# A two-block transformer kernel: stepped norm and late low-rank finishing in block one, 96-row products in block two

## The chip, the cores and the metric

The kernel runs on one core of one Trainium2 chip. The metric is the device time of one execution in microseconds, lower is better. The engines: TensorE (PE, with its weight loads as PEld), VectorE (DVE), ScalarE (ACT), GpSimd (POOL) and SyncE (SP), which only issues DMAs here. ACT and POOL can issue DMAs too.

## The reference, cut to what matters

Two transformer blocks run one after the other on x of 1024 tokens by 1024 columns, in float32. What the change touches of block one:

```
h = rms_norm(x, norm_in)
proj = h @ w_in            # dq dk dv dgate cq ckv kr mgate g_diff g_mla
cq = rms_norm(cq, mla_q_norm)             # 384 columns
q = cq @ w_uq              # 4 heads: 128 plain, 64 rotated columns
ckv = rms_norm(ckv, mla_kv_norm)          # 256 columns
kv = ckv @ w_ukv           # 4 heads: 128 of k, 128 of v
k_rope = apply_rope(kr, cos, sin)         # 64 columns for all heads
```

Two causal attentions over q, k, v follow, gated with silu(dgate) and silu(mgate). What it touches of block two (a recurrence over tokens beside a dilated attention, then a feed-forward part):

```
logw = -softplus(-(w0 + tanh(xw) @ w_up)) - 0.5     # xw: 32 columns
a = sigmoid(a0 + xa @ a_up)                         # xa: 32 columns
g = sigmoid(xg) @ g_up                              # xg: 96 columns
```

## The kernel before, in words

Every large product is taken in three: a float32 operand is split into a rounded part (hi) and the rest (lo), and `mm3` (L196) adds hi x hi, hi x lo and lo x hi in one PSUM bank. `split` (L174) makes hi on ACT and lo on DVE; with a gain it multiplies by it on the way. Weights pass through a raw tile (`wr`, two buffers) that SP loads, and a split tile (`w`, four buffers).

`block_one` (L442) first norms x. In each of two halves of 512 tokens, four tiles of 128 tokens are loaded on SP, their sums of squares taken on ACT (`sumsq`, L435), the reciprocal root on DVE and POOL (`rstd`, L167), and the tiles scaled on DVE (L466). `to_T` (L257) then makes, for each of 8 blocks of 128 columns, four PE transposes into one PSUM bank, from which ACT writes hi (L269) and DVE writes lo (L270) of hT. The banks for transposes follow `tp_tags` (L446): one bank "tp" and, twice in three, one of the two banks "pj", which the products use too.

`attention_one` (L484) then makes, in this order: the rope tables (L310, DVE and ACT's sine); lambda (four small loads, DVE and ACT's exponential, L501 to L512); the split weights Wc of cq and Wk of ckv and kr; the products for cq (L568), eight token blocks of 128 tokens with 8 x 3 products each (`proj_tok_steps`, L212); those for ckv and kr (L577); the gate of the second attention (`gate_tok(1)`, L534); then q's rotated part (`qrope`, L595), q and k of four heads and v (L609 to L614), which `spill` (L601) copies from PSUM to a tile `ev` (two buffers, pool `evs`) and SP stores in DRAM. Each block of cq and ckv goes through `finish` (L556): copy from PSUM on DVE (L165), sum of squares, norm (L562). After every fourth block `finish` calls `to_T` for all four tiles at once, with the norm's gain taken in at L269 and L270. After that come the products for the first heads and the attention, in which two streams of instructions are woven so that PE has products of the one while the other waits.

In block two `project_two` projects into the recurrence's inputs. It makes T (L1000 to L1007), 128 partitions of 1024 tokens: rows 0 to 31 tanh(xw) rounded, 32 to 63 its rest, 64 to 95 and 96 to 127 the same of xa. `rwkv_tokens` (L1017), run for four groups of 128 channels, loads the `up` weights (L1027 to L1033), splits them, and `up` (L1044) multiplies 64 rows of T with the rounded weights (twice the same 32 rows) and 32 rows with the rest: two products of 64 and 32 partitions in one bank, for decay (rows from 0) and for a (rows from 64), for each half of the tokens.

The order of instructions on each engine is set when the kernel is built. In block one, the order of the program gives the priority, and an instruction comes in when what it needs is ready by a model of the times. In block two (`run`, L1911), a planner orders the whole block by a simulated timeline. `weave` (L115) takes turns between two streams by their stated costs.

Of the kernel before, what the change touches and what calls it, by code (L numbers as in the profile page):

```python
# [86 lines left out]
class Build:  # L87
# [288 lines left out]
    def q_stack(self, x, m):  # L376

        nc = self.nc
        qs = self.work.tile([128, 2, 2, 2, 64], F32R, name="qs")
# [5 lines left out]
        def rest():  # L385
# [5 lines left out]
            q = self.work.tile([128, 2, 2, 128], F32R, name="qT")  # L391
# [50 lines left out]
    def block_one(self):  # L442
        nc, A, tc = self.nc, self.A, self.tc
        with ExitStack() as st:
            self.psum = self.pool(st, "ps1", bufs=2, space=PSUM)
            self.tp_tags = ["tp", "pj", "pj"]  # L446
# [6 lines left out]
            with tc.tile_pool(name="xa", bufs=8, reuse_waits="tile") as xp:  # L453
                cm = xp.tile([128, 128], F32, name="cm", bufs=1)
# [29 lines left out]
    def attention_one(self, st, hT):  # L484
        nc, A, tc = self.nc, self.A, self.tc
        self.rope_tables(self.pool(st, "rope"))
# [12 lines left out]


        lam = self.consts.tile([128, 1], F32, name="lam")  # L501
        lq = self.work.tile([128, 4, 64], F32, name="rp1")
        for i, n in enumerate(("diff_lambda_q1", "diff_lambda_k1", "diff_lambda_q2", "diff_lambda_k2")):
            nc.sync.dma_start(lq[:, i], rows(A[n]))
# [1444 lines left out]
```

## Time and profile before

| | us |
|---|---|
| median of 3 runs | 2550.12 |
| lowest and highest | 2544.97, 2550.53 |
| the profiled execution's own time | 2538.74 |
| its span in the trace | 2536.5 |
| PE busy in the span | 2380.1 (94%) |
| DVE, ACT, POOL busy | 1495.4 (59%), 1018.2 (40%), 284.7 (11%) |
| mean granted TensorE clock | 0.976 |

The busy share is a mean over stages with different limits. A wait matters where it is PE's; idle time of the other engines costs nothing by itself. In the trace's names "pj<-w,hT_hi" is a product into a tile pj from tiles w and hT_hi, and L199 is the line that issues it.

### The profile page before, as it was taken

Reading aid. Unit: us, or ns where it says so; the run is one execution under the profiler, and the core shown is the slowest. Engines: PE = TensorE matmul, PEld = TensorE weight load, DVE = VectorE, ACT = ScalarE, POOL = GpSimd, SP = SyncE. Lnnn points to the kernel's source line nnn. Section 1 sums busy time; section 2 is a strip of 40 time slices with the busy share of each in tenths; the row PEclk is TensorE's granted clock in tenths of the full one; section 3 lists DMA queues with packets and bytes.
Section 4 is the critical chain, followed back from the end, with each engine's and each line's share of the span. In section 5 each row is a group of like instructions: output and inputs, shape, how many; then the busy total and the mean of one; then the engine's idle time right before and its main releaser. Section 6 shows DMA issues by size and latency. Waiting matters only on the chain.

```text
span 2536.5 us, 38731 instructions
## 1 busy us (share of the span) xinstructions
PE 2380.1 (94%) x14288; PEld 2087.0 (82%) x14288; DVE 1495.4 (59%) x3183; ACT 1018.2 (40%) x2210; POOL 284.7 (11%) x678
## 2 busy tenths in 40 slices
PE   7898999999999899899998798989999999989997
PEld 6887999898887689778797788988997877778776
DVE  5432457454445644466474265757667666688888
ACT  4312344344443225333342254445666444433333
POOL 1000000000001000101111554531100000000001
PEclk9999999999999999899999898999999999999999
DMA  3134222222213531335367676543556444443222
GB/s 112 52 110 138 81 61 80 64 76 76 73 63 125 179 138 53 76 75 165 96 185 206 173 165 173 157 119 96 178 160 183 144 138 133 170 133 109 74 76 107
DMA packets 371597, 302.47 MB, mean 119 GB/s; under 512 B 126161, under 2 KB 305233, under 8 KB 371409
## 3 DMA queue, kind: packets, MB, share of 16 engines
q1 hardware_dynamic: 345296, 271.69, 36.1%
q10 hardware_dynamic: 25472, 26.22, 3.6%
q8 instruction: 113, 1.85, 0.3%
q0 software_dynamic: 640, 2.10, 0.2%
q14 instruction: 76, 0.61, 0.1%
HBM read 208.69 MB, written 91.23 MB: 118 GB/s over the span
## 4 chain that ended last, share of the span: by engine, by line
PE 68%; DMA 11%; DVE 9%; ACT 4%; issue 3%; POOL 3%; SPq 2%; ACTq 0%; DVEq 0%; POOLq 0%
PE pj L199 34%; PE x L199 7%; PE z L199 5%; PE y L199 4%; PE pv L426 4%; DMA wr<-w_ffn_up 3%; PE tp L254 3%; DVE w L181 2%; ACT w L163 1%; PE sc L686 1%; POOL U L1262 1%; POOL Ut L1260 1%; DMA v<-bkv_t 1%; DMA Al<-at_d 1%; PE Z L1314 1%
## 5 line engine op out<-in xcount | busy, mean ns | idle before, releaser
L199 PE MATMUL pj<-w,hT_hi 128*128 128x256 f32 (+2 forms) x2560 | 539.8, 305 | 17.6 <-ACT w L177 7.4
L199 PEld LDWEIGHTS pj<-w,hT_hi 128*128 128x128 f32 x2560 | 420.6, 192 | 27.0 <-ACT w L177 7.7
L199 PE MATMUL pj<-hT_hi,w 128*128 128x512 f32 (+1 forms) x1216 | 395.4, 400 | 10.3 <-DVE tg L830 7.2
L199 PE MATMUL pj<-w,hT_lo 128*128 128x256 f32 (+2 forms) x1280 | 383.8, 301 | 0.0
L181 DVE TENSOR_TENSOR w<-wr,w 128x1024 fp32r<-128x1024 f32 (+4 forms) x349 | 279.2, 826 | 138.8 <-ACT w L163 136.6
L163 ACT ACTIVATE w<-wr 128x1024 fp32r<-128x1024 f32 (+4 forms) x345 | 241.5, 736 | 253.4 <-PE z L199 66.4
L199 PEld LDWEIGHTS pj<-hT_hi,w 128*128 128x128 f32 (+1 forms) x1216 | 228.1, 189 | 62.5 <-ACT w L163 6.6
L199 PEld LDWEIGHTS pj<-w,hT_lo 128*128 128x128 f32 x1280 | 245.9, 192 | 0.6 <-issue 0.5
L199 PE MATMUL pj<-hT_lo,w 128*128 128x512 f32 (+1 forms) x608 | 241.9, 398 | 0.0
L172 POOL TENSOR_TENSOR rstd<-rs_t,mhalf 128x1 f32<-128x1 f32 x88 | 59.3, 679 | 1511.9 <-DVE rs_t L171 1462.6
L199 PE MATMUL z<-w 128*128 128x512 f32 x720 | 166.9, 392 | 4.7 <-DVE c L1824 3.7
L199 PE MATMUL y<-w 128*128 128x512 f32 x624 | 150.5, 400 | 14.6 <-ACT w L163 9.4
L199 PEld LDWEIGHTS z<-w 128*128 128x128 f32 x720 | 135.7, 189 | 34.5 <-issue 4.1
L199 PEld LDWEIGHTS y<-w 128*128 128x128 f32 x624 | 119.9, 194 | 43.9 <-ACT w L163 10.7
L199 PE MATMUL ua<-T,w 128*128 128x512 f32 x576 | 139.5, 393 | 6.8 <-DVE o L1756 3.6
L199 PEld LDWEIGHTS ua<-T,w 128*128 128x128 f32 x576 | 107.3, 188 | 33.9 <-issue 8.0
L199 PEld LDWEIGHTS pj<-hT_lo,w 128*128 128x128 f32 (+1 forms) x608 | 115.4, 190 | 23.1 <-issue 0.8
L403 DVE TENSOR_REDUCE mx<-sc 128x1 f32<-128x128 f32 (+7 forms) x96 | 70.8, 754 | 101.6 <-PE sc L411 101.1
L254 PE MATMUL tp<-ident,p 128*128 128x128 f32 x576 | 98.5, 278 | 7.2 <-ACT pt L163 6.2
L199 PE MATMUL x<-w,mix_hi 128*128 128x256 f32 x512 | 92.3, 284 | 0.0
L199 PE MATMUL x<-B,w 128*128 128x512 f32 x384 | 88.3, 390 | 0.0
L407 ACT ACTIVATE p<-sc,mx 128x128 f32<-128x128 f32 (+7 forms) x96 | 70.7, 740 | 36.1 <-DVE mx L404 34.2
(440 smaller groups left out, 4391.2 us busy)
## 6 DMA issues: line engine op xcount, KB each, us to landing
wr<-w_ffn_up SPq DMA_DIRECT2D x48, 512.0 KB, 4.8
wr<-u_d SPq DMA_DIRECT2D x32, 512.0 KB, 5.2
wr<-w_ffn_down SPq DMA_DIRECT2D x32, 512.0 KB, 4.9
wr<-w_in SPq DMA_DIRECT2D x28, 512.0 KB, 4.1
wr<-w_in_first SPq DMA_DIRECT2D x192, 64.0 KB, 2.0
u_d<-o SPq DMA_DIRECT2D x48, 256.0 KB, 3.8
tg<-tg_d SPq DMA_DIRECT2D x32, 256.0 KB, 3.0
x_d<-x SPq DMA_DIRECT2D x16, 512.0 KB, 3.7
```

Source lines behind the costliest of these rows:

```text
L163: self.nc.scalar.activation(out, in_, AF.Copy)
L172: nc.gpsimd.tensor_tensor(out, t, self.mhalf[:, :ss.shape[-1]], op=OP.pow)
L181: self.nc.vector.tensor_sub(lo, x, hi.bitcast(F32))
L199: self.nc.tensor.matmul(ps, a, b, start=start, stop=stop, **({"skip_group_check": True} if onto else {}))
L254: self.nc.tensor.transpose(tp[:, j * 128:j * 128 + 128], s, ident)
L403: nc.vector.tensor_reduce(mx, sc[:, :n], axis=AX, op=OP.max)
L407: nc.scalar.activation(p[:, :n], sc[:, :n], AF.Exp, bias=mx, scale=scale, accum_out=s)
L426: self.nc.tensor.matmul(o[:, :w], pts[j], V[:, j], start=j == 0, stop=j == nb - 1)
L686: nc.tensor.matmul(o, qn, KN[:, c0:c0 + w], start=True, stop=False)
L1260: nc.gpsimd.tensor_mul(tmp[:, :ni, :w], U[:, :ni, s:s + 1].to_broadcast([128, ni, w]), Al[:, s:s + 1, s + 1:].to_broadcast([128, ni, w]))
L1262: nc.gpsimd.tensor_sub(U[:, :ni, s + 1:], U[:, :ni, s + 1:], tmp[:, :ni, :w])
L1314: mm(ps[:, j * 128:j * 128 + 128], lhs(c), rhs(c, j), start=True, stop=True)
```

## The change

In block one, all eight x tiles are asked for at the start, four on SP's queue and four on ACT's. Only half 0 is normed and transposed first. The rest of the norm is a generator, `second`, that is advanced once after each token block of cq: the norm of two tiles, that of the other two, the transposes of four column blocks, those of the other four, then the causal mask's load. The rope tables follow after block 4, lambda after ckv. Transposes now use the one bank "tp" and the one bank "pv" by turns. `finish` returns a generator: its first step is the norm's multiplication, its second the transposes of this one block (three for cq, two for ckv, in one bank, then hi on ACT and lo on DVE). `proj_tok_steps` keeps such generators in a list and advances each once after every later token block; the list is handed from cq to ckv and to the gate. The gains of both norms are taken into the weights' split. Spills and `qrope` use a pool `lev` with five buffers of `ev` in place of `evs`. The attention's tiles qs, qT, gt and mo move to a second pool, `work2`; rope's and mla's pools change sides.

In block two, T is made in a scratch tile and four DMAs copy it into two tiles of 96 partitions (hi, lo, hi again). The weights are loaded three times (32 rows each; two rounded, one turned into the rest), so that `up` is one product of 96 partitions. The split of these weights is one ACT and two DVE instructions instead of two and two.

```diff
@@ to_T
-        for d in range(nd):
+        for d in range(d0, d0 + nd):
             def then(i, n, ps, d=d):
-                hi = hT[0][:, d0 + d, half * 512:half * 512 + 512]
-                lo = hT[1][:, d0 + d, half * 512:half * 512 + 512]
+                hi = hT[0][:, d, half * 512:half * 512 + 512]
+                lo = hT[1][:, d, half * 512:half * 512 + 512]
...
@@ block_one
-            self.tp_tags = ["tp", "pj", "pj"]
+            self.tp_tags = ["tp", "pv"]
...
+            slow, sx = ExitStack(), ExitStack()
+            low = self.pool(slow, "low")
+            xp = self.pool(sx, "xa", bufs=8)
+            xs = [xp.tile([128, D], F32, name="x") for _ in range(NT)]
+            for t in range(NT):
+                (nc.sync if t < 4 else nc.scalar).dma_start(xs[t], A["x"][0, t * 128:t * 128 + 128, :])
+
+            def norm(ts):
+                for t in ts:
+                    ss = self.small.tile([128, 1], F32, name="ss")
+                    self.sumsq(t, ss, D)
+                    r = self.norm_rows(ss, D)
+                    nc.vector.tensor_scalar(t, t, r, None, op0=OP.mult)
+
+            def second():
+
+                norm(xs[4:6])
+                yield
+                norm(xs[6:8])
+                yield
+                for d in (0, 4):
+                    self.to_T(xs[4:8], hT, 1, 4, lambda d: gain[:, d:d + 1], d)
+                    yield
+                cm = self.work.tile([128, 128], F32, name="kx")
                 nc.sync.dma_start(cm, A["c_causal"])
                 nc.vector.tensor_copy(self.causal, cm)
-                for half in range(2):
-                    ts = []
-                    for j in range(4):
-                        t = xp.tile([128, D], F32, name="x")
-                        r0 = (half * 4 + j) * 128
-                        nc.sync.dma_start(t, A["x"][0, r0:r0 + 128, :])
-                        ss = self.small.tile([128, 1], F32, name="ss")
-                        self.sumsq(t, ss, D)
-                        r = self.norm_rows(ss, D)
-                        nc.vector.tensor_scalar(t, t, r, None, op0=OP.mult)
-                        ts.append(t)
-                    self.to_T(ts, hT, half, 8, lambda d: gain[:, d:d + 1])
-            if "hT" in self.dbg:
-                for i in range(2):
-                    nc.sync.dma_start(self.dbg["hT"][i], hT[i].bitcast(F32))
-                return
-            self.attention_one(st, hT)
+                sx.close()
...
+            norm(xs[0:4])
+            self.to_T(xs[0:4], hT, 0, 8, lambda d: gain[:, d:d + 1])
+            self.attention_one(st, hT, second(), slow, low)
...
@@ attention_one
-        self.rope_tables(self.pool(st, "rope"))
...
+        def minus_lambda():
+            lq = self.work.tile([128, 4, 64], F32, name="rp1")
...
-                self.split(t[:, 0], t[:, 1], raw)
+                self.split(t[:, 0], t[:, 1], raw, None if gain is None else gain[:, k:k + 1])
...
+        mla = self.pool(st, "mla", side="right")
+        self.rpool = self.pool(st, "rope", side="right")
...
+            def finish(width, dst, tb, ps):
+
+                t = low.tile([128, 384], F32, name="c", bufs=5)[:, :width]
+                self.evac(t, ps[:, :width], "v")
+                ss = self.small.tile([128, 1], F32, name="ss")
+                self.sumsq(t, ss, width)
+                r = self.norm_rows(ss, width)
+                n, sl = width // 128, slice(tb * 128, tb * 128 + 128)
+
+                def then(i, k, ps):
+                    ps = ps.rearrange("p (d t) -> p d t", d=n)
+                    nc.scalar.activation(dst[0][:, :, sl], ps, AF.Copy)
+                    nc.vector.tensor_sub(dst[1][:, :, sl], ps, dst[0][:, :, sl].bitcast(F32))
+
+                def rest():
+                    nc.vector.tensor_scalar(t, t, r, None, op0=OP.mult)
+                    yield
+                    self.transposes([t[:, d * 128:d * 128 + 128] for d in range(n)], then)
+                return rest()
+
+            late = []
+            for tb, _ in enumerate(self.proj_tok_steps(hT, Wc, 384, lambda tb, ps: finish(384, cqT, tb, ps), late=late)):
+                next(second, None)
+                if tb == 4:
+                    self.rope_tables(self.rpool)
             Wk = w_cols(320, 2432)
-            group = []
-
-            def finish(width, gain, dst, tb, ps):
-                t = low.tile([128, 384], F32, name="c", bufs=5)
-                self.evac(t[:, :width], ps[:, :width], "v")
-                ss = self.small.tile([128, 1], F32, name="ss")
-                self.sumsq(t[:, :width], ss, width)
-                r = self.norm_rows(ss, width)
-                nc.vector.tensor_scalar(t[:, :width], t[:, :width], r, None, op0=OP.mult)
-                group.append(t)
-                if len(group) == 4:
-                    self.to_T(list(group), dst, tb // 4, width // 128, lambda d: gain[:, d:d + 1])
-                    group.clear()
-
-            self.proj_tok(hT, Wc, 384, lambda tb, ps: finish(384, qn_gain, cqT, tb, ps))
+            low2 = self.pool(s2, "low2")
+            ckT = [low2.tile([128, 2, S], F32R, name=n) for n in ("ck_hi", "ck_lo")]
...
+                g = finish(256, ckT, tb, ps)
+
+                def rest():
+                    next(g)
+                    stack()
+                    yield
+                    next(g, None)
+                return rest()
+
+            self.proj_tok(hT, Wk, 320, ckv, late=late)
+            minus_lambda()
+            for _ in gate_tok(1, late):
...
+            lev = self.pool(s2, "lev", bufs=5)
 
             def qrope(tb, ps):
-                t = self.evs.tile([128, 512], F32, name="ev")
+                t = lev.tile([128, 512], F32, name="ev")
...
+        self.work2 = self.pool(st, "work2", bufs=2)
...
@@ project_two
-                hi = c.tile([128, S], F32R, name="T%d" % i)[:m]
+                hi = (c if i else self.epool).tile([128, S], F32R, name="T2" if i else "e")[:m]
...
-                    self.T1 = hi
+
+                    self.T1 = [c.tile([96, S], F32R, name="T1%d" % j) for j in range(2)]
+                    for j, t in enumerate(self.T1):
+                        r = j * 64
+                        nc.sync.dma_start(t[0:64].bitcast(F32), hi[r:r + 64].bitcast(F32))
+                        nc.sync.dma_start(t[64:96].bitcast(F32), hi[r:r + 32].bitcast(F32))
...
@@ rwkv_tokens
-        raw = self.wraw.tile([128, self.wn], F32, name="wr")[:, 0:256].rearrange("p (a c) -> p a c", a=2)
-        for i, n in enumerate(("decay_up_2", "decay_up_2", "aaa_up_2", "aaa_up_2")):
-            self.load(raw[i * 32:i * 32 + 32, 0], self.A[n][0][:, ch])
-        self.load(raw[0:96, 1], self.A["gate_up_2"][0][:, ch])
-        wup, wupl = [self.rc.tile([128, 2, 128], F32R, name=x, bufs=2) for x in ("wup", "wupl")]
-        for x in ((slice(0, 128), 0), (slice(0, 96), 1)):
-            self.split(wup[x], wupl[x], raw[x])
+        raw = self.wraw.tile([128, self.wn], F32, name="wr")[0:96].rearrange("p (a c) -> p a c", a=3)
+        for j, n in enumerate(("decay_up_2", "aaa_up_2")):
+            for i in range(3):
+                self.load(raw[i * 32:i * 32 + 32, j], self.A[n][0][:, ch])
+        self.load(raw[:, 2], self.A["gate_up_2"][0][:, ch])
+        wup, wupl = [self.rc.tile([96, m, 128], F32R, name=x, bufs=2) for x, m in (("wup", 3), ("wupl", 1))]
+        nc.scalar.activation(wup, raw, AF.Copy)
+        nc.vector.tensor_sub(wup[64:96, 0:2], raw[64:96, 0:2], wup[64:96, 0:2].bitcast(F32))
+        nc.vector.tensor_sub(wupl[:, 0], raw[:, 2], wup[:, 2].bitcast(F32))
...
-        def up(r0, sl):
+        def up(j, sl):
             ps = self.bank("u")
-            mm(ps, wup[r0:r0 + 64, 0], self.T1[r0:r0 + 64, sl], start=True, stop=False)
-            mm(ps, wupl[r0:r0 + 32, 0], self.T1[r0:r0 + 32, sl], start=False, stop=True)
+            mm(ps, wup[:, j], self.T1[j][:, sl], start=True, stop=True)
             return ps
```

## Rows read from the trace of the kernel before

**Rows 1.** Stages: length, busy PE, PEld, DVE, ACT, POOL (instructions), clock, DMA share, GB/s.

```profile
0.00:32.50 32.50, 16.60 (x65) 11.68 (x65) 20.41 (x42) 22.37 (x37) 4.89 (x12) 1.00 0.58 186
32.50:114.10 81.60, 71.08 (x433) 68.13 (x433) 43.97 (x140) 26.51 (x66) 8.93 (x16) 0.98 0.16 44
228.30:700.00 471.70, 468.70 (x3282) 417.71 (x3283) 241.19 (x728) 188.78 (x505) 17.24 (x24) 1.00 0.25 73
1054.00:1372.00 318.00, 311.30 (x1636) 266.72 (x1634) 188.14 (x272) 109.65 (x192) 48.01 (x41) 0.99 0.50 135
1372.00:2536.50 1164.50, 1075.02 (x6273) 944.29 (x6273) 781.58 (x1513) 515.88 (x1031) 187.92 (x557) 0.96 0.47 139
```

**Rows 2.** PE's waits from 32.6 to 115 us: total, times, longest.

```profile
PE pj L254 <- DVE c L562: 4.2, 4, 1.5
PE pj L199 <- DVE cq_lo L270: 2.7, 2, 1.3
```

**Rows 3.** Stretches of 3.41 us, columns as in rows 1.

```profile
72.67:76.08 3.41, 0.62 (x4) 0.39 (x4) 2.28 (x5) 2.39 (x5) 0.55 (x1) 1.00 0.58 174
76.08:79.49 3.41, 3.41 (x13) 3.41 (x14) 2.41 (x3) 1.30 (x2) 0.00 (x0) 0.50 0.53 154
...
198.96:202.37 3.41, 3.41 (x10) 2.48 (x9) 0.69 (x1) 0.36 (x1) 0.00 (x0) 0.50 0.42 160
```

**Rows 4.** PE's waits from 160 to 228.3 us.

```profile
PE pj L199 <- DVE ev L165: 7.5, 6, 2.3
PE pj L199 <- ACT ev L163: 1.9, 3, 0.9
```

**Rows 5.** Timeline of ACT, 5 to 33 us: start, us, engine, line, operation.

```profile
6.21 1.06 ACT L437 ACTIVATE junk<-x 128x1024 bf16<-128x1024 f32 x1 [4.18 <-DMA x<-x]
...
10.13 1.06 ACT L437 ACTIVATE junk<-x 128x1024 bf16<-128x1024 f32 x1
...
32.55 0.84 ACT L163 ACTIVATE w<-wr 128x768 fp32r<-128x768 f32 x1
```

**Rows 6.** The page's part 6: DMA issues, count, KB, us to landing.

```profile
wr<-w_in_first SPq DMA_DIRECT2D x192, 64.0 KB, 2.0
```

**Rows 7.** The tile v_d: its stores, ns min/median/max, first and last start.

```profile
L108 SPq DMA_DIRECT2D v_d<-ev x32: 319/431/1549, 209.1 to 229.5; - x32
```

**Rows 8.** Timeline of PE at products of few rows, 1099, 1160 and 1241 us.

```profile
1099.58 0.50 PE L1046 MATMUL u<-T,wup 64*128 64x512 f32 x1
1100.01 0.50 PE L1047 MATMUL u<-T,wupl 32*128 32x512 f32 x1
...
1160.25 0.39 PE L199 MATMUL u<-T,wup 96*128 96x512 f32 x1
1160.48 0.39 PE L199 MATMUL u<-T2l,wup 96*128 96x512 f32 x1
...
1241.12 0.73 PE L1046 MATMUL u<-T,wup 64*128 64x512 f32 x2
```

**Rows 9.** Timeline of PE in the first 50 us.

```profile
13.54 0.69 PE L254 MATMUL pj<-ident,x 128*128 128x128 f32 x2 [0.65 <-DVE rs_t L171]
...
27.36 1.11 PE L254 MATMUL tp<-ident,x 128*128 128x128 f32 x4 [1.69 <-DVE hT_lo L270]
...
28.26 1.91 PE L254 MATMUL pj<-ident,x 128*128 128x128 f32 x8
32.49 0.62 PE L199 MATMUL pj<-w,hT_hi 128*128 128x384 f32 x2 [0.56 <-DVE hT_lo L270]
...
49.24 0.49 PE L254 MATMUL pj<-ident,c 128*128 128x128 f32 x3
...
49.57 0.49 PE L254 MATMUL tp<-ident,c 128*128 128x128 f32 x3
```

**Rows 10.** Groups of instructions up to 33 us: count, busy us, mean ns, idle before.

```profile
L269 ACT ACTIVATE hT_hi<-pj,cv_norm_in 128x512 fp32r<-128x512 f32 x11 | 7.2, 685 | 1.8 <-PE pj L254 1.8
L270 DVE SCALAR_TENSOR_TENSOR hT_lo<-pj,cv_norm_in,hT_hi 128x512 fp32r<-128x512 f32 x10 | 7.2, 746 | 0.9 <-ACT hT_hi L269 0.7
```

More of the change, by code (lines that the diff above doesn't have):

```diff
@@ L378, in q_stack @@
         nc = self.nc
-        qs = self.work.tile([128, 2, 2, 2, 64], F32R, name="qs")
+        qs = self.work2.tile([128, 2, 2, 2, 64], F32R, name="qs")
         xv = x.rearrange("p (m d) -> p m d", m=m)
@@ L390, in rest @@
                                         qs[:, i, s].rearrange("p a d -> p (a d)"), self.identr)
-            q = self.work.tile([128, 2, 2, 128], F32R, name="qT")
+            q = self.work2.tile([128, 2, 2, 128], F32R, name="qT")
             self.evac(q[:, :m].rearrange("p m s t -> p (m s t)"), tp[:, :m * 256].bitcast(F32))
@@ L482, in w_in, with attention_one @@
                 for k in range(c)]
-    def attention_one(self, st, hT):
+    def attention_one(self, st, hT, second, slow, low):
         nc, A, tc = self.nc, self.A, self.tc
-        self.rope_tables(self.pool(st, "rope"))
         qn_gain, kv_gain = self.colvec("mla_q_norm", 3), self.colvec("mla_kv_norm", 2)
@@ L501, in attention_one, with w_set @@
         lam = self.consts.tile([128, 1], F32, name="lam")
-        lq = self.work.tile([128, 4, 64], F32, name="rp1")
-        for i, n in enumerate(("diff_lambda_q1", "diff_lambda_k1", "diff_lambda_q2", "diff_lambda_k2")):
-            nc.sync.dma_start(lq[:, i], rows(A[n]))
-        lp = self.work.tile([128, 2, 64], F32, name="rp2")
-        nc.vector.tensor_mul(lp, lq[:, 0:4:2], lq[:, 1:4:2])
-        ls = self.small.tile([128, 2], F32, name="ls", bufs=1)
-        nc.vector.tensor_reduce(ls, lp, axis=AX, op=OP.add)
-        le = self.small.tile([128, 2], F32, name="le", bufs=1)
-        nc.scalar.activation(le, ls, AF.Exp)
-        nc.vector.tensor_sub(lam, le[:, 1:2], le[:, 0:1])
-        nc.vector.tensor_scalar(lam, lam, -(0.8 - 0.6 * math.exp(0.0)), None, op0=OP.add)
-        def w_set(pieces, n, nk, g):
+        def minus_lambda():
+            lq = self.work.tile([128, 4, 64], F32, name="rp1")
+            for i, n in enumerate(("diff_lambda_q1", "diff_lambda_k1", "diff_lambda_q2", "diff_lambda_k2")):
+                nc.sync.dma_start(lq[:, i], rows(A[n]))
+            lp = self.work.tile([128, 2, 64], F32, name="rp2")
+            nc.vector.tensor_mul(lp, lq[:, 0:4:2], lq[:, 1:4:2])
+            ls = self.small.tile([128, 2], F32, name="ls", bufs=1)
+            nc.vector.tensor_reduce(ls, lp, axis=AX, op=OP.add)
+            le = self.small.tile([128, 2], F32, name="le", bufs=1)
+            nc.scalar.activation(le, ls, AF.Exp)
+            nc.vector.tensor_sub(lam, le[:, 1:2], le[:, 0:1])
+            nc.vector.tensor_scalar(lam, lam, -(0.8 - 0.6 * math.exp(0.0)), None, op0=OP.add)
+        def w_set(pieces, n, nk, g, gain=None):
             W = []
@@ L542, in then @@
                     self.store(self.g_d[i][tb * 128:tb * 128 + 128, c * 256:c * 256 + 256], th)
-                yield from self.proj_tok_steps(hT, W, 256, then)
-        mla = self.pool(st, "mla")
+                yield from self.proj_tok_steps(hT, W, 256, then, late=late)
+        mla = self.pool(st, "mla", side="right")
+        self.rpool = self.pool(st, "rope", side="right")
         krs = mla.tile([128, S], F32R, name="krs")
-        with ExitStack() as s2:
-            low = self.pool(s2, "low")
+        with slow as s2:
@@ L602, in spill @@
                 n = ps.shape[-1]
-                t = self.evs.tile([128, 512], F32, name="ev")[:, :n]
+                t = lev.tile([128, 512], F32, name="ev")[:, :n]
                 self.evac(t, ps)
@@ L650, in gate @@
         def gate(i, qb, h):
-            g = self.work.tile([128, 128], F32, name="gt", bufs=4)
+            g = self.work2.tile([128, 128], F32, name="gt", bufs=4)
             nc.sync.dma_start(g, self.g_d[i][qb * 128:qb * 128 + 128, h * 128:h * 128 + 128])
@@ L701, in last @@
                         ps = product()
-                        o = self.work.tile([128, 128], F32, name="mo", bufs=5)
+                        o = self.work2.tile([128, 128], F32, name="mo", bufs=5)
                         nc.vector.scalar_tensor_tensor(o, ps, r, g, op0=OP.mult, op1=OP.mult)
@@ L737, in last @@
                         ps = product()
-                        o = self.work.tile([128, 128], F32, name="mo", bufs=5)
+                        o = self.work2.tile([128, 128], F32, name="mo", bufs=5)
                         nc.scalar.activation(o, ps, AF.Copy, scale=r1)
```

33 lines of the change are left out of this document (11 added, 22 removed).

## The prediction

> **What bounds the kernel now.** I read the busy times by stage first, to see where TensorE (PE) stands idle [rows 1]. From 228 to 700 us, the attention, PE works 468.7 of 471.7 us: whatever is saved ahead of it is saved at the end too, since nothing there waits for anything but PE. The two stretches before it are looser. In the first 32.5 us PE has 16.6 us of work, and from 32.5 to 114.1, where the low ranks cq and ck are made, 10.5 us of 81.6 are idle. In block two the stretch from 1054 to 1372, which holds the products with the low ranks of the recurrence, is PE's again (311.3 of 318.0). After that 89.5 us of 1164.5 are idle, so there a chain of other engines counts as well.
>
> Next come the waits of PE in the second stretch: 4.2 us for c (its norm, L562) and 2.7 for cq_lo, each in pieces of up to 1.5 us [rows 2]. They are one pattern: after four token blocks `finish` transposes four tiles at once, the last of which has just left PE, and PE walks through evacuation, sum of squares, norm and the second evacuation with nothing else to do. Then the clock [rows 3]: in the 3.4 us up to 76.08 PE was busy for 0.62 us, and in the next 3.4 us the granted clock is 0.50, 1.2 GHz of 2.4. So each long pause costs 1.7 us more. There are three such stretches before the attention (76, 114 and 199 us); the first two follow cq and ck.
>
> Third, the waits between 160 and 228 us [rows 4]: 7.5 and 1.9 us for `ev`, the tile that spilled heads are copied to. It has two buffers, and a buffer is free only when its store has landed.
>
> **The change, part by part.** The sums are made against the profiled execution, 2538.74 us (span 2536.5); the median of the runs shown, 2550.12, lies 11.4 above, and I carry the difference over unchanged.
>
> (a) *Late finishing of cq and ck.* The norm of a token block is now issued one block later and its transposes two blocks later, beside products that are ready; the list is not emptied between cq, ck and the gate. So the 10.5 us of idle time and two stretches at half clock (2 x 1.7) can go: 13.9. What is late next is Wk: its buffers come free only as the last block of cq passes, and its third tile waits for a raw buffer. That may cost 0 to 4 us at each of two borders by the nearest rows, a split of 0.84 us a tile [rows 5] and a load of 2.0 [rows 6]; DVE (44.0 of 81.6 us busy) may hold PE up here and there. I take 2.4 for all, as transposes and the first two thirds of the products lie over it: **11.5**, between 6 and 13.9. Moving the gain of the norm into the weight split costs one operation of the same form in place of another: nothing.
>
> (b) *Five buffers for the spills* (`lev`). The waits are 9.4 us and the half-clock stretch at 199 us 1.7, together 11.1. What is left is the SP queue: 32 stores of v at a median of 0.431 us are 13.8 us [rows 7], and PE has 8 x 6 products of 512 columns at 0.23, the step of 96-row products of that width [rows 8], 11.0. Five buffers let PE run up to 3 us ahead, and SP catches up under the products that follow. I take **9**, between 3 (SP sets the pace after all) and 11.1.
>
> (c) *The start.* Now all 64 transposes of x come first and the first product at 32.49 [rows 9]. In the change the products of token blocks 0 to 3 follow on half 0 alone, half 1 is stepped in between them, half 1 loads on ACT's queue, and transposes alternate between two PSUM banks instead of three. Two things delay half 0. The x tiles land 1.3 us apart (6.21 to 10.13 for three steps [rows 5]); if both queues share the engines evenly, the fourth tile of half 0 lands as late as the eighth does now, some 5 us later, and its transposes start at about 18.6 instead of 13.54 [rows 9]. No row shows two queues at the start, so the price is 0 to 5 us and I take 5. Then a bank is busy for 4 transposes (0.9), ACT's 0.69 and DVE's 0.75 [rows 9, 10] and about 0.6 of handing on, 2.95; with two banks a group takes 1.5 us, the six groups after the first two 8.9, and half 0 is done at about 29.5. Block 0's products go in between, as each needs one group, and end about 30.5. A block is 4.1 us (96 products in 16.75 [rows 9]), so this is as good as a start at 26.4. Half 1's 32 transposes then take 0.11 each, as those of c do, not 0.22 as those of x do now [rows 9]: 3.5. 32.49 - 26.4 - 3.5 is 2.6; I take **2**. Bounds: with no delay by the shared queues +7; with Wc's last split as late as now (33.4 [rows 5] and DVE's behind it) and one more block at the half clock -6.
>
> The Trainium skill (DMA: Bandwidth & Descriptors, Queues, rings and completion order) says that each DMA engine goes round the queues it has work for. By that the shared 5 us hold, as taken; without them this term would be +7.
>
> (d) *Rope tables, lambda, mask, `work2`.* Their DVE and ACT work moves behind the first products and DVE has room (44.0 of 81.6); uncovered, the tables would cost some 8 us once, which only the case on the start below could show. The lambda, mask and position loads leave SP's head and pass later, ahead of nothing that PE waits for. Lambda's exponential may reload ACT's tables once, and ACT has room (26.5 of 81.6): nothing. The 4 x loads on ACT's queue cost ACT 4 issues of about 0.5 us before its first tile lands: nothing. The duplicated pool changes places in SBUF, no instruction.
>
> (e) *The 96-row product.* Now an `up` is a 64-row and a 32-row product. Each holds PE 0.43 us from start to start, where a 96-row product of as many columns takes 0.23 [rows 8]. An `up` costs 0.85 and after the change 0.23; 16 of them give 9.9. The first one also starts 0.1 late after a full-row product, the pair at 1241 us overlapped in part (two in 0.73): together **10**, between 7 and 11.5. It counts while PE bounds the stretch, and it does [rows 1].
>
> The Trainium skill (TensorE: Matmul & The Clock Gate, Why this matters for your kernels) holds that a product of few rows takes as long as a full one and that products in separate row groups run side by side. By it an `up` would cost 0.46, the gain would be 3.7 and the chance of pairing would be lost; the rows disagree on the first and show the second once.
>
> Against it stand four copies between SBUF tiles that the first `up`, at 1099.58 [rows 8], now waits for. No row shows such a copy; by the nearest, a load that lands in 2.0 us [rows 6], and four issues it slips by 0 to 3 us. PE has the next projection meanwhile; behind the copies on SP stand weight loads of that projection. Eight more small loads pass on SP beside 192 of w_in_first: nothing while PE is full. I take 1 off: **9**.
>
> **Sum**: 11.5 + 9 + 2 + 9 = 31.5 us. 2538.7 becomes 2507.2, and the median 2550.1 becomes 2518.6, say 2519.
>
> **Rivals.**
> *The start loses* (0.14). The shared queues, two banks and Wc's late split together give term (c) its lower end, -6: 8 us less, 2526.6. For it: Wc's last split is at 33 us now, and ACT's work is not less. Against: PE has products to do in between.
> *Late products are late already* (0.08). Instructions are ordered by readiness when the kernel is built, so the new steps might leave PE's order much as it was: (a) falls away, 20 us are left, 2530. Against: PE stands [rows 2] although the next block's products needed nothing from c but a bank.
> *SP paces the spills* (0.05): (b) gives 3, 2524.6.
> *Few rows cost what many do* (0.03): the 0.43 belongs to the place and not to the rows, so that the 96-row product saves one product of 0.23 per `up`: 3.7 less 1, 2525. Against it: the 0.23 at 96 rows is of the same stretch [rows 8]. The Trainium skill (TensorE: Matmul & The Clock Gate, same section) says the first half of this.
> *The second block is planned anew and gives it back* (0.07). Its order comes from a planner that sees other costs; idle time after 1372 us is 89.5 us [rows 1], and a plan with a third more of it costs 30: 2549, no change that a measurement of this kernel can tell (0.2%, 5 us).
> *PE never gets to its full pace* (0.05, slower). Place: from the first products to the end of ck. Products on tiles that come one by one could be spread so thinly that PE stays as slow as it is now for x: its transposes take twice the step of those of c [rows 9], though the row of that stretch shows a granted clock of 1.00 [rows 1]. Price: a cq product at 0.174 would take as much again, 192 of them 33 us, and the 192 of ck (320 columns, 0.145) 28: 2518.6 + 61 = 2580. It decides once it outlasts the cq stage, where 33 eat up the sum of 31.5. Against: at half speed PE is the bound, so it would be busy without a pause, and now the first products, at 32.49, run at full pace after 3.6 us of nearly unbroken transposes.
>
> **How the numbers follow.** The forecast has 0.58, with the rivals 1.0. Faster by over 0.2%: the forecast and the four rivals on that side, 0.88. Within 0.2%: 0.07, the replanned block. Slower: 0.05. The range reaches up past 2530, to which the milder rivals come and two small misses together (2537), and down to where (a), (b), (c) and (e) are at their upper ends (2.4, 2.1, 5 and 1.5 us: 2508), with 5 more for a lucky plan: 2503 to 2538.
>
> **What would show it.** Right: the first cq product before 30 us; no wait of PE for c, cq_lo or ck_lo over 0.5; no stretch at clock 0.50 between 40 and 230 us; `ev` waits under 2 us; the gate's first product some 13 us earlier; the attention's start 20 to 25 us earlier; `up` as one product at 0.23. Wrong: a first product after 33, new waits for Wk, `up` waiting for its copies, or more idle time after 1372 us than 89.5.

## The result and the profile after

The changed kernel takes 2519.55 us (median of four runs, 2510.53 to 2522.37) beside 2547.55 for the kernel before on the same chip: a ratio of 0.9884, 95% interval 0.9855 to 0.9914. In a second series on another occasion it took 2514.92 beside 2551.08, 0.9861 (0.9846 to 0.9876). The forecast of 2519 holds as a sum. Its terms do not: the start lost time where it was to gain some, the spill buffers gave more than their bound, and the profiled execution of the kernel before misled the comparison behind the first Z product.

Starts of the same work in the traces, in us (read off PE's timeline; "again" is a second profile of the same kernel):

| first product of | before | before again | after | after again |
|---|---|---|---|---|
| cq | 32.5 | 32.6 | 26.9 | 26.7 |
| ck and kr | 76.0 | 78.1 | 75.7 | 75.3 |
| the gate | 114.1 | 116.1 | 110.2 | 109.5 |
| the rotated q | 161.6 | 164.9 | 157.0 | 156.3 |
| the work after v | 224.9 | 231.1 | 206.4 | 205.5 |
| the recurrence's tokens (`up`) | 1099.6 | 1101.6 | 1080.3 | 1075.5 |
| the recurrence (Z) | 1363.3 | 1367.2 | 1331.2 | 1326.1 |
| end of the last w_in_first product | 1423.4 | 1427.9 | 1393.9 | 1392.1 |
| end of the last Z product | 1754.3 | 1772.8 | 1732.7 | 1728.2 |
| span | 2536.5 | 2555.4 | 2516.7 | 2511.4 |

Up to the work after v the changed kernel repeats within 1 us and the kernel before within 6. In the second profile of the kernel before about nine stretches of 3.41 us up to there have a granted clock near 0.50, four of them at the start (23.2 to 36.8 us), and not three. So each gain over it is a range.

Stages of the changed kernel, columns as in [rows 1]:

```profile
0.00:26.90 26.90, 2.76 (x8) 1.16 (x8) 6.88 (x17) 8.80 (x14) 2.41 (x8) 1.00 0.65 220
26.90:110.20 83.30, 78.05 (x481) 74.52 (x482) 52.61 (x154) 38.25 (x86) 11.40 (x19) 0.98 0.14 37
...
157.00:206.40 49.40, 48.16 (x243) 40.27 (x242) 23.94 (x53) 14.26 (x22) 0.00 (x0) 1.00 0.64 199
```

One stretch inside the second row has half the clock:

```profile
48.00:51.40 3.40, 3.27 (x12) 3.17 (x13) 1.91 (x6) 1.37 (x2) 0.55 (x1) 0.50 0.00 0
```

The first product comes 5.6 us earlier, but ahead of it PE has worked for 2.8 us and stood for 24. The stretch from there to the gate is 83.3 us long, not shorter than the 81.6 of [rows 1]: it now holds most of the transposes of x too. PE's waits in it, answering to [rows 2]:

```profile
PE tp L254 <- DVE rs_t L171: 1.5, 1, 1.5
PE pj L199 <- DVE w L181: 1.1, 1, 1.1
PE pj L199 <- ACT w L163: 1.1, 1, 1.1
...
PE tp L371 <- DVE cq_lo L575: 0.4, 1, 0.4
```

Those for c are gone and 0.4 is left for cq_lo. In their place stand waits for half 1 of x (rs_t) and for Wk (w, both at the border to ck). The stretch at half clock, at 48.0 us, follows the waits for x; in the second profile of the changed kernel the same waits (1.5 and 0.5 us) are there and no such stretch. From 157 to 240 us no wait for `ev` is left (answer to [rows 4]):

```profile
PE pj L199 <- DVE rp L356: 1.2, 4, 0.4
PE tp L389 <- ACT qT L163: 0.5, 1, 0.5
PE pj L199 <- ACT b L163: 0.3, 1, 0.3
```

An `up` is one product (answer to [rows 8]; count, then min, median and max in ns), and no idle time stands ahead of the first one, so the four copies held up nothing:

```profile
L1080 PE MATMUL u<-T,wup x16: 391/395/396, 1080.3 to 1271.0; 96*128 96x512 f32 x16
```

### The profile page after: what moved, and what is told of

The parts are those of the page before. It is cut to its first block, busy times and chain, and to the rows that moved or that the text cites. A ratio compares the mean times of both kernels' runs of the same rounds, so it can differ in the third digit from the quotient of the medians.

```text
span 2516.7 us, 38738 instructions
## 1 busy us (share of the span) xinstructions
PE 2358.6 (94%) x14272; PEld 2084.2 (83%) x14272; DVE 1495.3 (59%) x3189; ACT 1019.2 (40%) x2212; POOL 287.6 (11%) x678
## 4 chain that ended last, share of the span: by engine, by line
PE 72%; DMA 10%; DVE 9%; ACT 4%; issue 3%; POOL 1%; SPq 1%; ACTq 0%; DVEq 0%; POOLq 0%
PE pj L199 34%; PE x L199 7%; PE z L199 5%; PE pv L426 4%; PE y L199 4%; PE tp L254 3%; DMA wr<-w_ffn_up 3%; DVE w L181 2%; PE Z L1347 1%; PE sc L713 1%; ACT w L163 1%; PE Z L1256 1%; PE ua L199 1%; PE sc L745 1%; DMA wr<-w_in 1%
## 5 line engine op out<-in xcount | busy, mean ns | idle before, releaser
L181 DVE TENSOR_TENSOR w<-wr,w 128x1024 fp32r<-128x1024 f32 (+4 forms) x339 | 273.2, 833 | 118.5 <-ACT w L163 117.7
L163 ACT ACTIVATE w<-wr 128x1024 fp32r<-128x1024 f32 (+4 forms) x335 | 236.0, 741 | 252.1 <-PE z L199 68.0
L199 PE MATMUL y<-w 128*128 128x512 f32 x624 | 150.9, 401 | 14.8 <-ACT w L163 7.9
L254 PE MATMUL tp<-ident,p 128*128 128x128 f32 x576 | 99.1, 281 | 11.3 <-ACT pt L163 10.6
L254 PEld LDWEIGHTS tp<-ident,p 128*128 128x128 f32 x576 | 69.7, 149 | 22.5 <-ACT pt L163 16.3
```

Of the source, the lines that this page charges most:

```text
L163: self.nc.scalar.activation(out, in_, AF.Copy)
L181: self.nc.vector.tensor_sub(lo, x, hi.bitcast(F32))
L199: self.nc.tensor.matmul(ps, a, b, start=start, stop=stop, **({"skip_group_check": True} if onto else {}))
L254: self.nc.tensor.transpose(tp[:, j * 128:j * 128 + 128], s, ident)
```

## The experiments

**The start.** Timelines of DVE and ACT in the changed kernel, where PE waits from 9.09 to 20.90 us for the second x tile:

```profile
14.69 0.15 DVE L507 TENSOR_SCALAR cv_diff_subln<-cv_diff_subln 128x1 f32<-128x1 f32 x1 [6.35 <-DMA cv_diff_subln<-diff_subln]
19.14 0.23 DVE L478 CAST causal<-kx 128x128 bf16<-128x128 f32 x1 [4.29 <-DMA kx<-c_causal]
...
20.09 0.76 DVE L465 TENSOR_SCALAR x<-x,rstd 128x1024 f32<-128x1024 f32 x1 [0.67 <-POOL rstd L172]
```

```profile
8.17 2.35 ACTq L458 DMA_DIRECT2D x<-x  x2
10.62 1.06 ACT L437 ACTIVATE junk<-x 128x1024 bf16<-128x1024 f32 x1 [3.89 <-DMA cv_mla_q_norm<-mla_q_norm]
...
18.00 0.84 ACT L163 ACTIVATE w<-wr 128x768 fp32r<-128x768 f32 x1 [6.22 <-DMA wr<-w_in]
18.74 1.04 ACT L437 ACTIVATE junk<-x 128x1024 bf16<-128x1024 f32 x1
```

DVE works in order, and ahead of the norm of x tile 1, whose sum of squares was done at 11.8, stand two operations on small vectors whose loads are late. ACT stands just so: ahead of the squares of x tile 2 is the split of Wc, which waits for its raw tile until 18.0. Ahead of the squares of tile 1 stand two issues of half 1's loads (ACTq, 8.17 to 10.52). Any of the three could be what holds the start.

`small_first`: mask and three vectors first on ACT's queue.

```diff
+            cm = self.work.tile([128, 128], F32, name="kx")
+            nc.scalar.dma_start(cm, A["c_causal"])
+            nc.vector.tensor_copy(self.causal, cm)
+            self.vecs = {}
+            for n, m in (("mla_q_norm", 3), ("mla_kv_norm", 2), ("diff_subln", 1)):
+                v = self.vecs[n] = self.consts.tile([128, m], F32, name="cv_" + n)
+                nc.scalar.dma_start(v, cols(A[n], 128, m))
             for t in range(NT):
...
-                cm = self.work.tile([128, 128], F32, name="kx")
-                nc.sync.dma_start(cm, A["c_causal"])
-                nc.vector.tensor_copy(self.causal, cm)
...
```

> The changed kernel, with the causal mask and the three small gain vectors loaded at the head of ACT's queue, before x, and their DVE work issued before the norms. Theory (DVE stands behind small loads: 6.35 us for diff_subln and 4.29 for the mask before the norm of x tile 1): that norm comes at about 12 us, not 20.1; PE's three pauses from 9 to 26 us (15.2 us) shrink to under 9; block 0's product ends 3 to 5 us earlier (about 32 instead of 36.0), the gate's first product 3 to 5 earlier (106 instead of 110.2); in all 3 to 5 us less than the changed kernel. Rival (ACT, not DVE, holds it: it waits 6.2 us for Wc's first raw tile, until 18.0, before the sums of squares of x tiles 2 and 3): tile 1's norm is early, but the last norm of half 0 stays at 24 to 25 us and the gate's first product within 1 us of 110.2.

Measured: tile 1 is normed at 11.6, block 0 of cq ends at 33.2 (35.8 in the changed kernel), the gate starts at 107.2, 3.0 earlier, the lower end of the theory; 2514.65 us, ratio 0.9866 (0.9851 to 0.9881), an interval that overlaps those of the changed kernel. DVE's waits were real, but ACT holds most. Its timeline there:

```profile
15.15 0.84 ACT L163 ACTIVATE w<-wr 128x768 fp32r<-128x768 f32 x1 [4.38 <-DMA wr<-w_in]
...
18.73 0.84 ACT L163 ACTIVATE w<-wr 128x768 fp32r<-128x768 f32 x1 [1.70 <-DMA wr<-w_in]
19.48 1.04 ACT L437 ACTIVATE junk<-x 128x1024 bf16<-128x1024 f32 x1
```

The x tile of the last row had landed at 11.67, 7.8 us before.

`x_later`: half 1 of x on SP's queue, behind the loads of Wc.

```diff
-            for t in range(NT):
-                (nc.sync if t < 4 else nc.scalar).dma_start(xs[t], A["x"][0, t * 128:t * 128 + 128, :])
+            def load_x(ts):
+                for t in ts:
+                    nc.sync.dma_start(xs[t], A["x"][0, t * 128:t * 128 + 128, :])
+            load_x(range(4))
+            self.load_x = load_x
...
             Wc = w_cols(384, 2048)
+            self.load_x(range(4, NT))
```

> The changed kernel, with the x tiles of half 1 loaded on SP's queue behind the loads of Wc instead of on ACT's queue. Theory of the prediction (two queues share the engines, and half 0 and Wc land later for it): Wc's first raw tile lands at about 13 us instead of 18, the sums of squares of x tiles 2 and 3 move from 18.7 and 20.5 to 14, the norm of tile 3 from 24.9 to about 20, unless DVE still waits for the mask. Rival (DVE's small loads hold it, the shared queues cost little): tile 1's norm stays at 19 to 21 us, PE's first unbroken transposes stay at 25 to 26, and the later half 1 costs blocks 4 and 5 of cq 0 to 4 us of new waits: gate's first product at 110 to 114.

Measured: far more than either theory said. The first product is at 15.9, the gate at 95.4, 14.8 earlier than in the changed kernel and 18.7 earlier than before; 2511.37 us, 0.9858 (0.9833 to 0.9884). ACT's timeline:

```profile
7.15 1.06 ACT L437 ACTIVATE junk<-x 128x1024 bf16<-128x1024 f32 x1 [0.21 <-DMA x<-x]
...
9.73 1.06 ACT L437 ACTIVATE junk<-x 128x1024 bf16<-128x1024 f32 x1
...
14.78 1.69 ACT L163 ACTIVATE w<-wr 128x768 fp32r<-128x768 f32 x2
```

All four squares of half 0 now come before the splits of Wc, and DVE's norms before the mask (cast at 25.9, later than ever, and nobody waits). Three things moved at once: loads land earlier with one queue (Wc's first tile at 14.55, while its split starts at 18.00 in the changed kernel), half 1's issues no longer stand in ACT's order (tile 1's squares start at 7.15, not 10.62), and the order of ACT and DVE, which is set when the kernel is built from modelled landings, came out well.

`small_first_x_later`: both edits (the small loads are first on ACT's queue, all x on SP's).

> Both edits to the start together. If the two limits stand one behind the other (DVE's small loads, then ACT's wait for Wc's raw tile): the four norms of half 0 follow one another by about 16 us, PE's transposes run without a long pause from about 10 us, block 0's product ends at 24 to 28 instead of 36.0, and the gate's first product at 100 to 104 instead of 110.2, so that term (c) gets back 6 to 10 us. If half 1 then comes late, 3 to 5 of these go again in waits for x before blocks 4 and 5. If the start is not limited by loads at all, nothing moves by more than 1 us.

Measured: gate at 99.8, 4.4 later than with `x_later` alone; 2513.34 us, 0.9862 (0.9845 to 0.9878). The small loads now delay x: the first transpose moves from 8.6 to 10.8, since DVE waits 5.8 us for diff_subln ahead of the first norm. With the queues right, they were in the right place.

Beside `small_first` this run shows what the queue does with the small loads in one place. Tile 3 of x lands at 11.34 instead of 11.67, and Wc's first split can start at 12.50 instead of 15.15, but the squares of tile 3 start at 11.44 instead of 19.48, and the gate 7.3 us earlier. So x itself lands hardly earlier, and ACT's order is the larger part. A kernel with the order alone changed was not run.

**The late finishing.** `at_once` issues norm and transposes with their own block.

```diff
-                def rest():
-                    nc.vector.tensor_scalar(t, t, r, None, op0=OP.mult)
-                    yield
-                    self.transposes([t[:, d * 128:d * 128 + 128] for d in range(n)], then)
-                return rest()
+                nc.vector.tensor_scalar(t, t, r, None, op0=OP.mult)
+                self.transposes([t[:, d * 128:d * 128 + 128] for d in range(n)], then)
...
```

> The changed kernel, with norm and transposes of cq and ck issued with their token block, not one and two blocks later (term a alone undone, but without the grouping by four). Theory (the late issue took the waits away): PE waits 0.5 to 1.5 us for c or its norm in most of the 16 blocks, 8 to 14 us between 27 and 110, and the gate's first product comes 8 to 14 us after 110.2. Rival (the order by readiness already puts the transposes behind other products when only the grouping by four is gone): fewer than 3 us of such waits, gate's first product within 3 us of 110.2.

Measured: gate at 114.0, 3.8 later; 2527.27 us, 0.992 (0.989 to 0.9951). PE's waits from 26 to 125 us begin with

```profile
PE pv L254 <- DVE c L577: 2.6, 5, 1.0
PE tp L254 <- DVE c L577: 2.6, 6, 0.6
```

It lies between the two theories. The late issue removes 5 us of waits for c. No stretch at half clock is left from 26 to 125 us here, although the issue is not late: to undo the grouping by four was enough against the long pauses.

**The spill buffers.** `two_buffers`:

```diff
-            lev = self.pool(s2, "lev", bufs=5)
+            lev = self.pool(s2, "lev", bufs=2)
```

> The changed kernel with two buffers for the spills instead of five. Theory (the buffers alone made the gain from 157 to 206 us, larger than the bound of 11.1 that the prediction gave, since transposes moved out of this stretch too): the waits for the spill buffer are back at 8 to 10 us, with one stretch at half clock, and from the first q product to the first product after v it takes 60 to 61 us, not 49.4. Rival (part of the gain came from the weights now loaded and split earlier, not from the buffers): waits of 4 to 7 us and 54 to 58 us. In all 5 to 11 more than the changed kernel.

Measured: 64.9 us from the first q product (155.7) to the work after v (220.6), beside 49.4; 2539.04 us, 0.9973 (0.9957 to 0.9989), so that most of the change's gain is gone. Theory (60 to 61) and rival (54 to 58) were both too low for the stretch, and so was the 5 to 11 for the total (19 to 24 above the changed kernel's two series). PE's waits from 157 to 245 us:

```profile
PE pj L199 <- DVE ev L165: 9.7, 7, 3.2
PE pj L199 <- ACT ev L163: 1.8, 2, 0.9
```

The buffers alone are worth 15.5 us up to there. 11.3 are PE's idle time, nearly all in these waits, and the stretch at half clock behind them costs 1.7; the rest is in PE's busy time, told at the end. Why the totals lie further apart than the stretch stays open.

**The 96-row product.** `lowrank_alone` is the kernel before with block two's part of the change, `block_one_alone` the change without it (the diffs are the two halves of the change's own).

> The kernel before with only the 96-row product (term e). In the changed kernel the stretch from the first low-rank product to the first Z product is 12.9 us shorter, but the recurrence from there to the last Z product is 10.5 longer (391.0 to 401.5). Theory (the product itself brings on what the recurrence gives back: that stage is bound by loads and the inverse, not by PE, or its new order waits): first low-rank product to first Z 250 to 252 us instead of 263.7, recurrence 398 to 406, total 1 to 6 us under the kernel before. Rival (the give-back comes from the earlier arrival of all the rest, or from the run): recurrence at 391 plus or minus 3, and the whole 9 to 13 us are kept in the total.

> The changed kernel with the product of block two as it was before (terms a to d alone). Theory (block one's gain is carried through, since nothing after it waits for time): the first product after v at 206 to 207 us instead of 224.9, first low-rank product about 19 earlier than 1099.6, recurrence 391 plus or minus 3 from first to last Z, total 17 to 21 us under the kernel before. Rival (an earlier block one is itself given back in the recurrence): recurrence 398 or more, and the total only 7 to 12 under the kernel before.

Measured: `lowrank_alone` 2541.61 us, 0.9983 (0.9967 to 0.9998), 4.3 under the kernel before; first `up` to first Z 251.1 us, recurrence 407.5. `block_one_alone` 2526.37, 0.9925 (0.99 to 0.9951), 19.6 under; first `up` to Z 263.8, recurrence 397.5, not the 391 of the theory, which rested on the one profile of the kernel before. So block one's gain is kept, and of the product's 12.8 us to the first Z a third arrives in the total. Part of the 12.8 was never gained: between the first Z product and the last with w_in_first lie 174 products of w_in_first without the edit and 188 to 192 with it (191 in the changed kernel). The 17 more, at a step of 0.174 us, are 3.0 us of work pushed behind the milestone. 9.8 is the real size.

`mv_ahead`. The largest wait of the recurrence after the change, and its counterpart before, in PE's waits:

```profile
PE Z L1256 <- DMA MV<-kr_d: 11.2, 1, 11.2
```

```profile
PE Z L1223 <- DMA MV<-kr_d: 1.9, 1, 1.9
```

```diff
+        self.rwkv_load2(n, p, hf)
+        if n + 1 < len(self.units):
+            self.rwkv_load1(n + 1, *self.units[n + 1])
         Al = self.Al[n] = self.ipool.tile([128, 32, 32], F32, name="Al", bufs=2)
         nc.sync.dma_start(Al.rearrange("p s t -> p (s t)"),
...
-        self.rwkv_load2(n, p, hf)
-        if n + 1 < len(self.units):
-            self.rwkv_load1(n + 1, *self.units[n + 1])
```

> The changed kernel, with one issue moved: the load of Al (512 KB, spread from a scratch tensor) stands behind the next unit's loads of BK, MV and v on SP's queue, not before them. In the kernel before, MV of the second unit stood ahead of Al, in the changed one behind it. Theory (the 11.2 us that PE waits for this MV at 1350.7, with half a clock behind it, are most of the 10.5 us that the recurrence gives back, and come from that order): the wait falls under 2 us, and the last Z product ends 7 to 11 us earlier than 1732.7; the total is 7 to 11 less than the changed kernel. Rival (the recurrence is bound by its loads of dq and by the inverse on POOL, which now gets Al later): the wait goes, but PE waits as much more for dq or RHS, and the last Z product and the total stay within 3 us.

Measured: 2516.93 us, 0.9873 (0.9854 to 0.9891); the last Z product ends at 1734.9, not earlier. The waits that stand in its place:

```profile
PE Z L1347 <- DVE RHS L1356: 12.6, 1, 12.6
PE sc L1218 <- DMA dq<-dqk_d: 11.5, 2, 9.1
PE Z L1347 <- ACT HN L1363: 6.4, 2, 5.7
...
PE Z L1267 <- DMA v<-bkv_t: 5.6, 1, 5.6
...
PE Z L1256 <- DMA MV<-kr_d: 2.7, 1, 2.7
```

My theory falls, and the rival holds: 8.5 us of this wait go, and v (no wait in the changed kernel), RHS (9.3 there) and HN (0.9 there) take them back. dq does not: over both its lines (L1218, L1219) it stands at 15.5 beside 15.7.

**Is it given back at all?** `before_again` and `after_again` are the two kernels unchanged, `x_later_again` is `x_later`, and `x_later_no_lowrank` is that without the 96-row product.

> The kernel before, unchanged, profiled a second time. Its profiled execution (2538.7) lay 9 us under its other runs. Theory (the recurrence of that one execution was a lucky one, and part of what the changed kernel seems to give back there is this): the stretch from the last product with w_in_first to the last Z product takes 335 to 340 us, not 331.0, and the total is 2543 to 2550. Rival (the stretch is the same in every execution of the kernel before, and the change made it longer): 331 plus or minus 1.5. What is fixed by the program, the products of w_in_first between first Z and the last of them, is 174 again by both.

> The changed kernel, unchanged, beside the next two on the same chip. By its first runs 2519.6, about 28 under the kernel before. From its start to the attention the profile repeats (first cq product at 26 to 28, gate 109 to 111, attention 238 to 241); from the first Z product on it may differ by up to 6 us.

> The changed kernel with half 1 of x behind Wc's loads on SP's queue, again, with more runs. Theory (15 us gained at the start stay, since PE bounds everything up to the recurrence): 10 to 16 us under the changed kernel of the same call. Rival (what comes earlier is given back in the recurrence, which is bound by its loads): 3 to 9 us under it.

> The last one with the product of block two as it was before (term e undone). Theory (of the 12.7 us that the product gains up to the first Z product, 3.0 are 17 products of w_in_first pushed behind it, and 3 to 6 more go in waits for loads in the recurrence): 174 such products after the first Z instead of 188 to 192, first low-rank product to first Z 263.7, and 3 to 7 us slower than with the 96-row product. Rival (the product keeps its 9.7 us): 8 to 12 us slower.

Measured: `before_again` 2557.68 us. The stretch from the last w_in_first product to the last Z, in the kernel before and then in its second profile:

```profile
1423.40:1754.30 330.90, 291.54 (x2366) 280.50 (x2365) 204.44 (x729) 153.42 (x419) 144.30 (x452) 0.94 0.59 152
```

```profile
1427.90:1772.80 344.90, 295.13 (x2366) 285.19 (x2366) 205.09 (x729) 153.17 (x419) 143.71 (x450) 0.93 0.57 145
```

The same program, the same 2366 products, and 14.0 us between them, more than the 335 to 340 us that I had expected. In the changed kernel it took 338.8 and again 336.1. So my reading that the change makes the recurrence longer rested on one execution at the low end; its rival, 331 in every execution, falls.

`after_again` took 2514.92 us, `x_later_again` 2510.63 (2507.02 to 2511.34), 0.9842 (0.9827 to 0.9857), and `x_later_no_lowrank` 2508.91, 0.9841 (0.9824 to 0.9857). Half 1 behind Wc beats both kernels: 4.3 us under the changed one, whose four runs (2513.31 to 2517.18) all lie above its five. But the gate was 12.7 us earlier than in `after_again`. Of these, 12.7 are left at the attention's start, 9.2 at the first `up`, 9.5 at the last Z, 8.3 at the start of the stage behind the recurrence and 6.3 at the end. So the rival's size (3 to 9) comes, but not its place, the recurrence: the loss comes in pieces of 1 to 3 us in several other stages, and what takes them stays open.

So does the net worth of the 96-row product, and both theories of `x_later_no_lowrank` (3 to 7 or 8 to 12 us slower) miss: the work is 8.3 us shorter from the first `up` to the last w_in_first product (316.6 against 324.9), but the totals say 4.3 on the kernel before, 7 to 11 between `block_one_alone` and the changed kernel (from different series), and nothing here. From the first `up` to the last Z the ten profiles with the product take 656.3 us in the mean (652.4 to 662.0) and the four without it 662.0 (654.8 to 671.2). The mean gain of 5.7 lies inside the spread.

## Why the prediction was right, and where it was not

The direction and the size hold: late finishing came near its term, the spill buffers above and the start below theirs. By the prediction's steps:

- **(a) and (c), 13.5 together: 4.6 at the first product of the rotated q, 8.6 in the second pair of profiles.** The shares are my estimate, from block 0 of cq: it ends at 35.8 beside 36.8, but half 1's transposes are still to come (3.5, at 0.11 each as forecast), and with them 2.0 us of waits for x and 1.7 of half clock. That puts (c) at -6.2 and (a) at 10.8; the second pair (36.5 beside 38.8, no half clock) gives -3.2 and 11.8.
- **(a), 11.5,** is right in its mechanism and, by this estimate, in its size: no wait for c, 0.4 for cq_lo, the stretches at half clock behind cq and ck gone; and the waits for Wk at the border, 1.1 twice, are as it put them (2.4).
- **(c), 2: the step that failed.** By the estimate above the rival "the start loses" came near its price of -6; its sum did not come, since (b) gave more. "Half 0 is done at about 29.5", and block 0 at 30.5: block 0 ended at 35.8, since the transposes of tile 1 came at 20.9 and those of tiles 2 and 3 later. The cause was named as engines shared by two queues (5 us); by the pair of runs above that is 0.3 for x and some 2.6 for Wc. ACT's order, the split of Wc ahead of the squares of tiles 2 and 3, was not looked at. The 1.3 us between tiles, from which the 5 were made, is ACT's own step (the squares at 10.13 in [rows 5] start without a wait) and no landing; the 413 to 426 GB/s at which the tiles of 512 KB came give about the same. And under (d) "the 4 x loads on ACT's queue cost ... nothing": they are issued from 5.59 to 10.52, not before the first tile lands, with the squares of tile 1 behind them. With the queue put right (`x_later`), both terms give 18.7 at the gate, inside the upper bounds of 13.9 and 7.
- **(d), nothing: it cost some 3 us,** which are part of the start's loss above. "Ahead of nothing that PE waits for" was wrong for the mask, which stands in DVE's order ahead of x's norms, and so does diff_subln, which the prediction does not name (`small_first`). In `x_later`, in the same places, they cost DVE 0.5 us.
- **(b), 9 of at most 11.1: 13.9 here (63.3 to 49.4 us), 17.0 in the second pair (66.1 to 49.1), 15.5 by `two_buffers`.** SP did not set the pace: the 48 products of v take 11.0 us (195.4 to 206.4), which is PE's own time for them by the forecast. The bound was wrong: it counted idle time and clock only, and a wait also breaks the overlap of the products around it.
- **(e), 9: 9.8 at the first Z** when the 3.0 us of moved work are taken off. The step of 0.62 times 16 was right. The pair at 1241 does not show products side by side, as the prediction reads it: two products in 0.73 us, of which the second takes 0.39 by itself, start 0.34 apart, more than the 0.23 of full-row ones. The copies cost nothing, but PE waits 2.4 us in the same stage for a DVE operation (L1154) that the faster products now run into (in `lowrank_alone` too). What of it arrives at the end stays open (above).
- **The second block planned anew (0.07).** Its sign, more idle time behind the first Z, showed in the first pair of profiles, and by `before_again` it is inside the spread of one kernel.
- **PE never at full pace (0.05).** It is at 0.32 a product until 30.9 us, and at 0.174 from there: some 2 us, no more.

Of the signs that it named, the first cq product (26.9), the waits for c, those for `ev` and the single `up` product came; the gate came 3.9 us earlier and not 13, one stretch at half clock was left (at 48 us, none in the second profile), and the attention came 18.4 us earlier, not 20 to 25. Of the signs against it the waits for Wk came. That 2519 was met to a microsecond is luck, from errors that cancel: 31.5 - 8.9 + 4.9 + 0.8 is 28.3 with (e) taken at the first Z, and the kernel before ran 2.6 us lower beside it than in the runs shown. The second series, with 36.2, shows how far it could have been off.

## What to carry to other kernels

When loads are moved to another queue, look at every engine's order behind them: one operation on a late tile holds all that stands behind it, and here an order that put a weight's split before the first norms cost more than the transfer. A wait on a buffer can cost PE its idle time, the clock behind it, and the overlap of the products that it separates, so that a bound made of idle time alone is too low. Profile the kernel before twice before a stage of it is compared: a stage bound by loads here differed by 14 us between two executions, and the stages before the attention by 6.

## What was not expected of the hardware

PE's busy time itself grows with waits. Over the same stretch (157 to 206 us of the changed kernel above, and 155.7 to 220.6 of `two_buffers`) with 243 and 242 instructions:

```profile
155.70:220.60 64.90, 52.39 (x242) 40.59 (x240) 24.58 (x54) 15.24 (x24) 0.00 (x0) 0.97 0.57 176
```

52.4 against 48.2: 1.7 are the half clock, and 2.5 are left, about 0.28 us for each of its 9 waits for `ev`. Two products behind such a wait, and two elsewhere in `two_buffers`:

```profile
203.42 0.73 PE L199 MATMUL pj<-w,ck_hi 128*128 128x512 f32 x2 [0.97 <-DVE ev L165]
...
204.91 0.62 PE L199 MATMUL pj<-w,ck_hi 128*128 128x512 f32 x2
```

That is 0.11 more behind the wait. Ahead of it the last product (0.39) has no successor 0.23 after its start, another 0.16. Both together are 0.27. The ends of PE's products are modelled in the profile, so the split between idle and busy time is an estimate; the 15.5 us between the two stretches are not.

A load can stand long behind another of its queue. In the changed kernel Al (512 KB) was issued at 1349.63 and its first reader started at 1360.55; MV, issued next at 1350.32, let PE start at 1361.87. The wait of 11.2 us comes again in the second profile (11.4). With MV ahead of Al it was 1.9 us in the kernel before and 2.7 in `mv_ahead`, where v stands behind Al and is waited for (5.6).
